# A two-layer hybrid decoder on one core: down tiles and input-projection parts laid out so that the last four activations come later, and ada loads issued ahead

## The chip, the cores and the metric

The kernel runs on one core of a Trainium2 chip. The time is device time in microseconds of one execution. Three runs of the kernel before took 996.03, 997.90 and 997.75 us, median 997.75. The engines named below are TensorE (PE, with its weight loads as PEld), VectorE (DVE), ScalarE (ACT), GpSimd (POOL) and SyncE (SP), which issues nearly all loads.

## What is computed

Two layers, 256 tokens of width 1024, all in float32. Each layer is a half-step SwiGLU, a mixer of latent attention and a gated short convolution, and another half-step SwiGLU. Each sublayer's norm is modulated by shift, scale and gate, which come from the conditioning vector c through a matrix w_ada of 9 x 1024 columns per layer:

```python
def swiglu(h, w_gu, w_down):
    g, u = jnp.split(h @ w_gu, 2, axis=-1)
    return (jax.nn.silu(g) * u) @ w_down

c_act = jax.nn.silu(c)
for l in range(DEPTH):
    mod = jnp.split(c_act @ w_ada[l] + b_ada[l], N_MOD, axis=-1)
    h = modulate(rms_norm(x, ffn1_norm[l]), mod[0], mod[1])
    x = x + FFN_RESIDUAL * (1 + mod[2])[:, None, :] * swiglu(h, ffn1_w_gu[l], ffn1_w_down[l])
    h = modulate(rms_norm(x, mix_norm[l]), mod[3], mod[4])
    y = hybrid_mixer(h, cos, sin, w_in[l], q_a_norm[l], w_uq[l], kv_a_norm[l], w_ukv[l],
                     conv_w[l], attn_out_norm[l], conv_out_norm[l], w_o[l])
    x = x + (1 + mod[5])[:, None, :] * y
    h = modulate(rms_norm(x, ffn2_norm[l]), mod[6], mod[7])
    x = x + FFN_RESIDUAL * (1 + mod[8])[:, None, :] * swiglu(h, ffn2_w_gu[l], ffn2_w_down[l])
return rms_norm(x, final_norm)
```

## The kernel before

**Weights.** All weights come in chunks of 128 x 2048 float32 (1 MB), 16 tiles of 128 x 128. A chunk is loaded by SP into `raw`, copied by ACT to `hi` in the matmul's reduced float format (L262), and VectorE forms `lo` = raw - hi (L265). TensorE then makes each product in three passes: hi by hi, hi by lo, lo by hi, all recorded at L287. The activations are split in the same way: `u` is the modulated norm's input of a sublayer (hi at L351 on ACT, lo at L357 on VectorE), `a` the SwiGLU product between gate/up and down (L351, L355). raw, hi and lo have three buffers each, PSUM has four.

**Sublayers.** An ffn takes 22 gate/up chunks, one per 128 columns of gate and of up, and then 11 down chunks: 8 output blocks (m0 to m7), each a sum over 22 activation blocks (k0 to k21), 22 tiles per block. When a block is summed, VectorE adds it to x with a gate (residual, L394), and ACT and VectorE form the next sublayer's u of that block at once, and its square for the norm's sum (acc, L322). The mixer follows a list, ORDER, of parts: K, Q, P, c and d are parts of the input projection of four tiles each (d the last columns of the convolution), q, s, t and a belong to attention, A and B to the output projection, N, Z, V, X, L, v to the latent's expansion, m and n are the sums of the two output norms, and w means that the next weight chunk is taken up here, ahead of its use.

**Modulation.** The product with w_ada is made on VectorE: 144 blocks of 128 rows, 512 KB each, are loaded by SP into `ada` (four buffers) and reduced by one instruction each (L189). A table, PACE, says how many must be done by which weight chunk.

**What sets the order.** SP's program order is written out: for each chunk its raw load and then the ada loads that PACE wants by then; inside the mixer TensorE's order is also written out. On VectorE and ACT a scheduler orders the work by due times (`due`), which run with TensorE's modelled clock, and by when it expects its inputs. Each engine executes in its own order, so whatever stands behind a waiting instruction waits too. The lines that the steps below touch are `load` (L235 to L276), `ffn` (the loop over `KD * NJ` tiles), `proj` (parts of four tiles), the output projection's residuals and the packing of dn and win.

Of the kernel before, what the change touches and what calls it, by code (L numbers as in the profile page):

```python
# [18 lines left out]
P = 128  # L19
L = 2  # L20
D = 1024
S = 256
KD = D // P
# [8 lines left out]
CH = 16 * P  # L32
WHOLE = 4
ADA_SLACK = 10000
ROPE_SLACK = 20000
LATE = 4
PACE = (0, 0), (8, 16), (21, 32), (33, 58), (49, 64), (84, 97), (117, 130), (133, 136), (146, 144)
LOAD_LEAD, SPLIT_LEAD, URGENT = 12000, 3000, 0
ENGS = {'p': mybir.EngineType.PE, 's': mybir.EngineType.SP, 'v': mybir.EngineType.DVE, 'a': mybir.EngineType.Activation}
MAN = 'sp'  # L40
SM_ACT = 2
ORDER = ("K K K X K Q Q P Q Q P P L c c c P c N Z V v q0 q1 s0 q2 c c c c t0 s1 a0 q3 c c c t1 c a1 s2 s3 c c c c t2 d d a2 t3 d d a3 "
         "d n w d w d d A A A w m A A w A A A B B B B B B B B").split()
WIN = dict(K=0, Q=1, P=2, c=3, d=7)
WO = dict(A=0, B=2)
SLACK = {'B': 6000, 'K': -2000, 'L': -4000, 'N': 0, 'P': 6000, 'Q': 0, 'V': 1000, 'X': 6000, 'Z': -4000, 'a': -4000, 'c': 6000, 'd': 0, 'm': 6000, 'n': 0, 'q': 2000, 's': -6000, 't': -4000}
# [1 line left out]
GUARD = ('m',)  # L48
MIX_SPLIT, MIX_ADA = 2000, 2000
GU_SLACK, DN_SLACK = 3000, 4000  # L50
NA = 72
SCALE = 96.0 ** -0.5
NEG = -1.0e30
# [66 lines left out]
def trunk(ctx: ExitStack, tc, x_d, c_d, pos_d, small_d, cst_d, ada_d, gu1_d, dn1_d, win_d, up_d, wo_d, gu2_d, dn2_d, out_d):  # L120
# [89 lines left out]
    stream = []  # L210
    for l in range(L):
        stream += [(gu1_d[l, j], CH, 2, WHOLE * P if l == 0 and j < 8 else 0) for j in range(NJ)]
        stream += [(dn1_d[l, j], CH, 2) for j in range(11)]
        up = {t: (up_d[l, :, a:a + n], n, 2) for t, a, n in (("N", 0, CH), ("q0", CH, 1536), ("q2", CH + 1536, 768),
                                                           ("q3", CH + 2304, 768))}
        n = {}
        for t in ORDER:
            n[t] = n.get(t, -1) + 1
            if t in up:
                stream.append(up[t])  # L220
            elif t in WIN and n[t] % 4 == 0:
                stream.append((win_d[l, WIN[t] + n[t] // 4], CH, CUTS))
            elif t in WO and n[t] % 4 == 0:
                stream.append((wo_d[l, WO[t] + n[t] // 4], CH, CUTS))
        stream += [(gu2_d[l, j], CH, 2) for j in range(NJ)]
        stream += [(dn2_d[l, j], CH, 2) for j in range(11)]
    taken = [0]

    ready = []
# [5 lines left out]
    def load(apart=False, head=False):  # L235


        i = taken[0]
        taken[0] += 1
        src, n, cuts = stream[i][:3]  # L240
        z0 = stream[i][3] if len(stream[i]) > 3 else 0
        raw = wp.tile([P, CH], F32, tag="raw", name=nm("raw"), bufs=3)
        hi = wp.tile([P, CH], F32R, tag="hi", name=nm("hi"), bufs=3)
        lo = wp.tile([P, CH], F32R, tag="lo", name=nm("lo"), bufs=3)
        if head:
            ada_load(1)
            nc.sync.dma_start(raw[:, :z0], src[:, :z0])
            ada_load(2)
            nc.sync.dma_start(raw[:, z0:n], src[:, z0:n])
        else:  # L250
            due(-LOAD_LEAD)
            nc.sync.dma_start(raw[:, :n], src)
            due(lead[1])
            with ExitStack() as es:
                for q in guard:
                    es.enter_context(tc.issue_after(q))
                ada(ada_target(i + 1))
        c = (n - z0) // cuts
        zs = [slice(z0 + q * c, z0 + (q + 1) * c) for q in range(cuts)]

        def top(q):
            nc.scalar.activation(hi[:, zs[q]], raw[:, zs[q]], AF.Copy)  # L262

        def rest(q):
            nc.vector.tensor_tensor(lo[:, zs[q]], raw[:, zs[q]], f32(hi[:, zs[q]]), ALU.subtract)  # L265

        if apart:
            return (raw, hi, lo), top, rest
        with ExitStack() as es:
            for q in guard:  # L270
                es.enter_context(tc.issue_after(q))
            for q in range(cuts):
                due(c / 128 * 322 * q - lead[0])
                top(q)
                rest(q)
        return raw, hi, lo  # L276
# [127 lines left out]
    def ffn(l, sub, pre, nxt, first=False):  # L404
# [132 lines left out]
                evac(j, pt[:, 0, :S], pt[:, 1, :S], None)  # L537
        if nxt is None:
            y = [wk.tile([P, 4, S], F32, tag="ada", name=nm("y"), bufs=4) for _ in range(2)]
        for t in range(KD * NJ):  # L540
            m, k = divmod(t, NJ)
            if t % 16 == 0:
                w = chunk()
            if k == 0:
                ps = ps_tile()[:, 0, :]
            if m < KD - 1:
                mm3w(ps, w, t % 16, aB[k], aH[k], k == 0, k == NJ - 1)
            else:
                mm3(ps, w, t % 16, aH[k], aL[k], k == 0, k == NJ - 1)
            if k == NJ - 1:  # L550
                due(DN_SLACK if m < KD - 1 else -URGENT)
                residual(ps, m, l, sub, 0.5, m < KD - 1)
                if nxt is None:
                    if m == KD - 1:
                        psf = ps_tile()[:, 0, :S]
                        fin.sums(psf, True, False)
                        due(-URGENT)
                        fin.acc = None
                    fin.add(x[:, m, :])
                    nc.scalar.activation(y[m // 4][:, m % 4, :], x[:, m, :], AF.Copy, scale=small[:, L * SM_L + m:L * SM_L + m + 1])  # L560
                    if m == KD - 1:
                        last_norm(psf, y)
                else:
                    nxt.put(m)
                    if m == 5:
                        nxt.shifts()

    def mixer(l, pre, nxt):
# [35 lines left out]
        def proj(t, evac):  # L604

            n = seen[t] = seen.get(t, -1) + 1
            if n % 4 == 0:
                open_[t] = chunk(), ps_tile()
            w, pt = open_[t]
            i = n % 4 // 2  # L610
            for k in range(n % 2 * 4, n % 2 * 4 + 4):
                mm3(pt[:, i, :], w, i * KD + k, uH[:, k, :], uL[:, k, :], k == 0, k == KD - 1, 2)
            if n % 4 == 3:
                due(SLACK[t])
                evac(scaled(pt))
# [163 lines left out]
        def out(t):  # L779
# [13 lines left out]
                dst = acc[m // 2 % 2][:, g, (m % 2) * S:(m % 2 + 1) * S]  # L793
                mm3(dst, w, m % 4 * 4 + k, zH[:, k, :], zL[:, k, :], half == 0 and k == 0 and m % 2 == 0, half == 1 and k == 3)
            if half == 1 and i % 2 == 1:
                due(SLACK["B"])
                for q in (i - 1, i):
                    m = 4 * g + q
                    residual(acc[m // 2 % 2][:, g, (m % 2) * S:(m % 2 + 1) * S], m, l, 1, 1.0)
                    nxt.put(m)  # L800
                    if m == 5:
                        nxt.shifts()
# [101 lines left out]
def _layout(a):  # L904
# [18 lines left out]
    for f in (1, 2):  # L923
# [3 lines left out]
            head = w[0, :8].reshape(8, P, 8, 2, P).transpose(2, 1, 0, 3, 4).reshape(1, 8, P, CH)  # L927
            w = np.concatenate([np.concatenate([head, w[:1, 8:]], axis=1), w[1:]], axis=0)
        g[f"gu{f}"] = np.ascontiguousarray(w)
        t = _tiles(a[f"ffn{f}_w_down"]).transpose(0, 2, 1, 3, 4).reshape(L, 11, 16, P, P)  # L930
        g[f"dn{f}"] = np.ascontiguousarray(t.transpose(0, 1, 3, 2, 4).reshape(L, 11, P, CH))
    w = a["w_in"]
    kv, kpe, q = w[:, :, QR:QR + KVR], w[:, :, QR + KVR:QR + KVR + 32], w[:, :, :QR]
# [3 lines left out]
    for i, s in [(i, s) for i in range(4) for s in (1, 2)] + [(i, 0) for i in range(4)]:  # L937
        parts.append(w[:, :, o + s * CW + i * P:o + s * CW + (i + 1) * P])
    t = _tiles(np.concatenate(parts, axis=2))
    t = t.transpose(0, 2, 1, 3, 4).reshape(L, 9, 16, P, P)  # L940
    g["win"] = np.ascontiguousarray(t.transpose(0, 1, 3, 2, 4).reshape(L, 9, P, CH))
    uk = a["w_ukv"].reshape(L, 2, P, H, 128)
    nope = uk[..., :64].reshape(L, 2, P, 4, P).transpose(0, 2, 3, 1, 4).reshape(L, P, 1024)
# [30 lines left out]
```

## Time and profile before

| what | value |
|---|---|
| median of three runs | 997.75 us |
| the profiled execution's own time | 1002.27 us |
| span of its profile | 1000.5 us |
| TensorE busy | 977.1 us, 98% |
| VectorE busy | 854.1 us, 85% |
| ACT busy | 581.3 us, 58% |
| granted TensorE clock, mean | 0.994 |
| loads | 248.59 MB, 250 GB/s over the span |

The profile is one execution, and its time lies 1.8 us over its span and 4.5 us over the median. Layer 0's first ffn takes the first 205 us, with its down from 144; the mixer is from 205 to 312; the second ffn to 501; layer 1 repeats this, with its mixer from 689 and its second ffn from 801. The release named behind an idle time is inferred from semaphores. In a row of a timeline the first number is the start in us, the second the duration; operations that follow each other without a gap are put together, with xN.

### The profile page before, as it was taken

Reading aid. Unit: us, or ns where it says so; the run is one execution under the profiler, and the core shown is the slowest. Engines: PE = TensorE matmul, PEld = TensorE weight load, DVE = VectorE, ACT = ScalarE, POOL = GpSimd, SP = SyncE. Lnnn points to the kernel's source line nnn. Section 1 sums busy time; section 2 is a strip of 40 time slices with the busy share of each in tenths; the row PEclk is TensorE's granted clock in tenths of the full one; section 3 lists DMA queues with packets and bytes.
Section 4 is the critical chain, followed back from the end, with each engine's and each line's share of the span. In section 5 each row is a group of like instructions: output and inputs, shape, how many; then the busy total and the mean of one; then the engine's idle time right before and its main releaser. Section 6 shows DMA issues by size and latency. Waiting matters only on the chain.

```text
span 1000.5 us, 16812 instructions
## 1 busy us (share of the span) xinstructions
PE 977.1 (98%) x6560; PEld 898.1 (90%) x6560; DVE 854.1 (85%) x1598; ACT 581.3 (58%) x1010; POOL 8.0 (1%) x27
## 2 busy tenths in 40 slices
PE   9999999999999999999999999998999999999996
PEld 7999998899989988888998888888998998888885
DVE  5899999999999998988899878877799999766653
ACT  4465544467856755654486555543687676656541
POOL 0000110000000000000000000000000000000000
PEclk9999999999999999999999999998999999999998
DMA  9999998874746687877768777776355547655531
GB/s 348 376 361 340 336 320 324 311 282 154 275 178 253 234 318 253 301 267 291 270 219 324 279 258 283 277 255 214 124 217 193 200 171 290 215 178 201 173 122 43
DMA packets 47007, 250.78 MB, mean 251 GB/s; under 512 B 5504, under 2 KB 5824, under 8 KB 26576
## 3 DMA queue, kind: packets, MB, share of 16 engines
q1 hardware_dynamic: 46224, 248.81, 68.3%
q8 instruction: 51, 0.84, 0.3%
q10 hardware_dynamic: 288, 0.65, 0.2%
q0 software_dynamic: 416, 0.25, 0.1%
q14 instruction: 28, 0.23, 0.1%
HBM read 248.59 MB, written 1.10 MB: 250 GB/s over the span
## 4 chain that ended last, share of the span: by engine, by line
PE 78%; DVE 11%; DMA 7%; issue 1%; ACT 1%; SPq 0%; DVEq 0%; ACTq 0%
PE ps L287 78%; DMA ada<-in_ada 6%; DVE lo L265 5%; DVE ada L189 1%; DVE x L394 1%; DMA raw<-in_gu 1%; DVE acc L322 1%; DVE u L357 1%; PE ps L731 1%; DVE mr L355 1%; ACT hi L262 0%; DMA cb<-in_c 0%; DVE nt L594 0%; ACT mr L351 0%; DVE mf L767 0%
## 5 line engine op out<-in xcount | busy, mean ns | idle before, releaser
L287 PE MATMUL ps<-u,hi 128*128 128x256 f32 (+2 forms) x2464 | 599.8, 324 | 6.5 <-ACT u L351 3.7
L287 PE MATMUL ps<-u,lo 128*128 128x256 f32 (+1 forms) x1664 | 470.1, 283 | 1.1 <-DVE lo L265 1.1
L287 PEld LDWEIGHTS ps<-u,hi 128*128 128x128 f32 x2464 | 413.5, 190 | 46.4 <-ACT u L351 4.3
L265 DVE TENSOR_TENSOR lo<-raw,hi 128x1024 fp32r<-128x1024 f32 (+2 forms) x384 | 394.8, 1046 | 41.4 <-ACT hi L262 40.9
L262 ACT ACTIVATE hi<-raw 128x1024 fp32r<-128x1024 f32 (+2 forms) x384 | 338.3, 912 | 113.4 <-PE ps L287 48.9
L287 PEld LDWEIGHTS ps<-u,lo 128*128 128x128 f32 x1664 | 315.9, 190 | 1.4 <-DVE lo L265 1.4
L287 PE MATMUL ps<-a,hi 128*128 128x512 f32 (+1 forms) x792 | 248.6, 372 | 1.4 <-DVE a L355 1.4
L189 DVE CUSTOM_DVE_ANT_0 ada<-ada,cb,small 128x1024 f32<-128x1024 f32 x144 | 183.1, 1280 | 33.4 <-DMA ada<-in_ada 32.8
L287 PE MATMUL ps<-a,lo 128*128 128x256 f32 x704 | 197.9, 281 | 0.0
L287 PEld LDWEIGHTS ps<-a,hi 128*128 128x128 f32 x792 | 143.0, 189 | 29.8 <-DVE a L355 1.7
L287 PEld LDWEIGHTS ps<-a,lo 128*128 128x128 f32 x704 | 133.2, 189 | 0.0
L351 ACT ACTIVATE a<-cc 128x256 fp32r<-128x256 f32 x88 | 36.3, 415 | 68.0 <-DVE cc L413 56.3
L287 PE MATMUL ps<-mr,hi 128*128 128x256 f32 x384 | 70.6, 285 | 0.0
L351 ACT ACTIVATE u<-x,gs 128x256 fp32r<-128x256 f32 x40 | 20.3, 507 | 84.6 <-DVE x L394 84.6
L287 PEld LDWEIGHTS ps<-mr,hi 128*128 128x128 f32 x384 | 60.2, 192 | 0.8 <-issue 0.3
L287 PE MATMUL ps<-mr,lo 128*128 128x256 f32 x192 | 54.3, 283 | 0.0
L394 DVE SCALAR_TENSOR_TENSOR x<-ps,gate,x 128x256 f32<-128x256 f32 x76 | 35.9, 480 | 19.2 <-PE ps L287 18.5
L355 DVE TENSOR_TENSOR a<-cc,a 128x256 fp32r<-128x256 f32 x88 | 37.0, 422 | 16.0 <-ACT a L351 15.8
L412 ACT ACTIVATE cc<-g 128x256 f32<-128x256 f32 x54 | 22.5, 418 | 41.5 <-DVE g L411 41.5
L411 DVE TENSOR_TENSOR g<-ps,g 128x512 f32<-128x512 f32 x54 | 37.0, 685 | 0.7 <-ACT g L410 0.6
L287 PEld LDWEIGHTS ps<-mr,lo 128*128 128x128 f32 x192 | 36.8, 191 | 0.0
L410 ACT ACTIVATE g<-ps 128x512 f32<-128x512 f32 x54 | 31.2, 578 | 0.0
(121 smaller groups left out, 568.4 us busy)
## 6 DMA issues: line engine op xcount, KB each, us to landing
raw<-in_gu SPq DMA_DIRECT2D x87, 1024.0 KB, 5.8
ada<-in_ada SPq DMA_DIRECT2D x144, 512.0 KB, 6.2
raw<-in_dn SPq DMA_DIRECT2D x44, 1024.0 KB, 5.2
raw<-in_win SPq DMA_DIRECT2D x18, 1024.0 KB, 5.7
raw<-in_wo SPq DMA_DIRECT2D x8, 1024.0 KB, 4.8
raw<-in_up SPq DMA_DIRECT2D x2, 1024.0 KB, 5.9
raw<-in_up SPq DMA_DIRECT2D x2, 768.0 KB, 4.4
raw<-in_up SPq DMA_DIRECT2D x4, 384.0 KB, 3.1
```

Source lines behind the costliest of these rows:

```text
L189: nc.vector.tensor_tensor_reduce(out=a, in0=a, in1=cb, scale=1.0, scalar=sm(l, t), op0=ALU.mult, op1=ALU.add, accum_out=mods[l][:, t:t + 1])
L262: nc.scalar.activation(hi[:, zs[q]], raw[:, zs[q]], AF.Copy)
L265: nc.vector.tensor_tensor(lo[:, zs[q]], raw[:, zs[q]], f32(hi[:, zs[q]]), ALU.subtract)
L287: nc.tensor.matmul(dst, a, b, **kw)
L322: nc.vector.tensor_tensor(self.acc, self.acc, t, ALU.add)
L351: nc.scalar.activation(dH, src, AF.Copy, scale=scale)
L355: nc.vector.tensor_tensor(dL, src, f32(dH), ALU.subtract)
L357: nc.vector.scalar_tensor_tensor(dL, src, scale, f32(dH), ALU.mult, ALU.subtract)
L394: nc.vector.scalar_tensor_tensor(x[:, m, :], s, g, x[:, m, :], ALU.mult, ALU.add)
L410: nc.scalar.activation(t2, pg[:, :, :S], AF.Copy)
L411: nc.vector.tensor_tensor(t2, pg[:, :, S:], t2, ALU.add)
L412: nc.scalar.activation(sg, t2[:, 0, :], AF.Silu)
```

## The change

Five edits. A chunk's ada loads stand ahead of its raw load on SP, and reach two blocks further than PACE asks (ADA_AHEAD). Down's tiles are in a new order: m0 and m1 first sum k0 to k17, then both k18 to k21; the other blocks as before. The weights are packed to suit. A down chunk is split by one operation of 2048 columns on ACT and on VectorE, no longer two of 1024. In the input projection, the first two parts of a chunk now take k0 to k3 of both its column blocks and the last two k4 to k7, also packed to suit; in ORDER, two Q parts stand between the second and the third K, and further on one w is dropped and the d parts move behind a3. Last, the residuals that are wanted at once get a due time 1500 earlier (URGENT), the output projection's last pair among them.

```diff
+ADA_AHEAD = 2
-LOAD_LEAD, SPLIT_LEAD, URGENT = 12000, 3000, 0
+LOAD_LEAD, SPLIT_LEAD, URGENT = 12000, 3000, 1500
-ORDER = ("K K K X K Q Q P Q Q P P L c c c P c N Z V v q0 q1 s0 q2 c c c c t0 s1 a0 q3 c c c t1 c a1 s2 s3 c c c c t2 d d a2 t3 d d a3 "
-         "d n w d w d d A A A w m A A w A A A B B B B B B B B").split()
+ORDER = ("K K Q Q K X K Q Q P P P L c c c P c N Z V v q0 q1 s0 q2 c c c c t0 s1 a0 q3 c c c t1 c a1 s2 s3 c c c c t2 d d a2 t3 d a3 "
+         "d d n d w d d A A A w m A A w A A A B B B B B B B B").split()
+DOWN = [(m, k) for k0, k1 in ((0, 18), (18, NJ)) for m in (0, 1) for k in range(k0, k1)] + [
+    (m, k) for m in range(2, KD) for k in range(NJ)]
...
-        stream += [(dn1_d[l, j], CH, 2) for j in range(11)]
+        stream += [(dn1_d[l, j], CH, 1) for j in range(11)]
...
             due(-LOAD_LEAD)
+            if not apart:
+                ada_load(min(ada_target(i + 1) + ADA_AHEAD, len(ADA_ORDER)))
             nc.sync.dma_start(raw[:, :n], src)
...
-        for t in range(KD * NJ):
-            m, k = divmod(t, NJ)
+        pd = {}
+        for t, (m, k) in enumerate(DOWN):
             if t % 16 == 0:
                 w = chunk()
             if k == 0:
-                ps = ps_tile()[:, 0, :]
+                pd[m] = ps_tile()[:, 0, :]
+            ps = pd[m]
...
-            i = n % 4 // 2
-            for k in range(n % 2 * 4, n % 2 * 4 + 4):
-                mm3(pt[:, i, :], w, i * KD + k, uH[:, k, :], uL[:, k, :], k == 0, k == KD - 1, 2)
+            i, h = n % 2, n % 4 // 2
+            for k in range(4 * h, 4 * h + 4):
+                mm3(pt[:, i, :], w, 4 * (n % 4) + k % 4, uH[:, k, :], uL[:, k, :], k == 0, k == KD - 1, 2)
...
-                due(SLACK["B"])
+                due(SLACK["B"] if n < 7 else -URGENT)
```

Three places show how the instructions move. The first is SP's queue at gate/up chunk 8 of layer 0 (`raw_84`), the first chunk to which the new order of loads applies. Before:

```order
26 L252 DMA raw_70_592<-in_gu1 128x2048
27 L252 DMA raw_84_687<-in_gu1 128x2048
28 L180 DMA ada_87_691<-in_ada 128x1024
29 L252 DMA raw_90_752<-in_gu1 128x2048
30 L180 DMA ada_93_756<-in_ada 128x1024
```

Now three ada loads stand ahead of it. The third needs a buffer that VectorE's reduction of ada_68 frees:

```order
26 L257 DMA raw_70_592<-in_gu1 128x2048
27 L183 DMA ada_87_690<-in_ada 128x1024
28 L183 DMA ada_88_692<-in_ada 128x1024
29 L183 DMA ada_89_694<-in_ada 128x1024
30 L257 DMA raw_84_687<-in_gu1 128x2048
31 L183 DMA ada_95_759<-in_ada 128x1024
```

VectorE at the same place, where lo_86 is the lo of that chunk, cc and `a` are the evacuations of the chunk before it, and L192 are reductions. Before, lo_86 stood right behind lo_72 and ahead of the first cc. Now:

```order
79 L270 TENSOR_TENSOR lo_72_594<-raw_70_592,hi_71_593 128x768
80 L421 TENSOR_TENSOR cc_76_647<-ps_18_157,cc_76_647 128x256
81 L192 ISA ada_88_692,mod0_88<-ada_88_692,cb_72,small_73 128x1024
82 L192 ISA mod0_88 128x1
83 L360 TENSOR_TENSOR a_74_645<-cc_76_647,a_74_645 128x256
84 L421 TENSOR_TENSOR cc_77_652<-ps_18_157,cc_77_652 128x256
85 L421 TENSOR_TENSOR cc_78_657<-ps_19_158,cc_78_657 128x256
86 L192 ISA ada_89_694,mod0_88<-ada_89_694,cb_72,small_73 128x1024
88 L360 TENSOR_TENSOR a_74_645<-cc_77_652,a_74_645 128x256
89 L360 TENSOR_TENSOR a_74_645<-cc_78_657,a_74_645 128x256
90 L421 TENSOR_TENSOR cc_79_662<-ps_19_158,cc_79_662 128x256
91 L270 TENSOR_TENSOR lo_86_689<-raw_84_687,hi_85_688 128x1024 x2
```

The chunk's split has moved behind two reductions and the evacuations of four columns.

The second is VectorE in layer 0's first down, at the first residual (m0: it adds ps_183 before, ps_185 now; each residual is two instructions, one to x and one more with the same gate for the other half of the products). lo_194 is down chunk 2 in both, lo_202 before and lo_204 now chunk 3. Before:

```order
249 L265 TENSOR_TENSOR lo_194_1779<-raw_192_1777,hi_193_1778 128x1024
250 L381 TENSOR_TENSOR u_75<-mod0_88,u_75 128x8
251 L394 SCALAR_TENSOR_TENSOR x_71<-ps_183_1688,gate_189_1747,x_71 128x256 x2
252 L265 TENSOR_TENSOR lo_202_1836<-raw_200_1834,hi_201_1835 128x1024
253 L357 SCALAR_TENSOR_TENSOR u_75<-x_71,gs_2_91,u_75 128x256
254 L265 TENSOR_TENSOR lo_202_1836<-raw_200_1834,hi_201_1835 128x1024
255 L189 ISA ada_203_1838,mod0_88<-ada_203_1838,cb_72,small_73 128x1024
```

Now:

```order
249 L270 TENSOR_TENSOR lo_194_1770<-raw_192_1768,hi_193_1769 128x2048
250 L192 ISA ada_206_1837,mod0_88<-ada_206_1837,cb_72,small_73 128x1024
251 L192 ISA mod0_88 128x1
252 L377 SCALAR_TENSOR_TENSOR gs_3_92<-mod0_88,small_73 128x1
253 L399 SCALAR_TENSOR_TENSOR x_71<-ps_185_1690,gate_197_1796,x_71 128x256
254 L270 TENSOR_TENSOR lo_204_1834<-raw_202_1832,hi_203_1833 128x2048
255 L399 SCALAR_TENSOR_TENSOR x_71<-ps_185_1690,gate_197_1796,x_71 128x256
256 L399 SCALAR_TENSOR_TENSOR x_71<-ps_191_1739,gate_199_1813,x_71 128x256
257 L192 ISA ada_210_1879,mod0_88<-ada_210_1879,cb_72,small_73 128x1024
```

The chunk's lo still follows the residual of m0, but that residual now needs down's tile 40, where it needed tile 22.

The third is VectorE where layer 1 goes from down to the mixer. lo_969 before and lo_963 now is the second chunk of the mixer, and the residual of ps_943 or ps_945 is down's last, m7. Before:

```order
1077 L265 TENSOR_TENSOR lo_969_7511<-raw_967_7509,hi_968_7510 128x512 x4
1078 L189 ISA ada_989_7657,mod1_89<-ada_989_7657,cb_72,small_73 128x1024
1079 L189 ISA mod1_89 128x1
1080 L394 SCALAR_TENSOR_TENSOR x_71<-ps_943_7331,gate_948_7409,x_71 128x256
1081 L265 TENSOR_TENSOR lo_973_7548<-raw_971_7546,hi_972_7547 128x512 x2
1082 L357 SCALAR_TENSOR_TENSOR u_75<-x_71,gs_701_5560,u_75 128x256
```

Now:

```order
1055 L192 ISA ada_991_7594,mod1_89<-ada_991_7594,cb_72,small_73 128x1024
1056 L192 ISA mod1_89 128x1
1057 L270 TENSOR_TENSOR lo_963_7404<-raw_961_7402,hi_962_7403 128x512 x4
1058 L399 SCALAR_TENSOR_TENSOR x_71<-ps_945_7271,gate_950_7347,x_71 128x256
1059 L270 TENSOR_TENSOR lo_979_7525<-raw_977_7523,hi_978_7524 128x512 x2
1060 L362 SCALAR_TENSOR_TENSOR u_75<-x_71,gs_703_5520,u_75 128x256
```

The reduction stands ahead of the second chunk's lo, no longer between it and the last residual.

More of the change, by code (lines that the diff above doesn't have):

```diff
@@ L225, in trunk @@
         stream += [(gu2_d[l, j], CH, 2) for j in range(NJ)]
-        stream += [(dn2_d[l, j], CH, 2) for j in range(11)]
+        stream += [(dn2_d[l, j], CH, 1) for j in range(11)]
     taken = [0]
@@ L929, in _layout @@
         g[f"gu{f}"] = np.ascontiguousarray(w)
-        t = _tiles(a[f"ffn{f}_w_down"]).transpose(0, 2, 1, 3, 4).reshape(L, 11, 16, P, P)
+        t = _tiles(a[f"ffn{f}_w_down"])
+        t = np.stack([t[:, k, m] for m, k in DOWN], axis=1).reshape(L, 11, 16, P, P)
         g[f"dn{f}"] = np.ascontiguousarray(t.transpose(0, 1, 3, 2, 4).reshape(L, 11, P, CH))
@@ L939, in _layout @@
     t = _tiles(np.concatenate(parts, axis=2))
-    t = t.transpose(0, 2, 1, 3, 4).reshape(L, 9, 16, P, P)
+    t = t.transpose(0, 2, 1, 3, 4).reshape(L, 9, 2, 2, 4, P, P).swapaxes(2, 3).reshape(L, 9, 16, P, P)
     g["win"] = np.ascontiguousarray(t.transpose(0, 1, 3, 2, 4).reshape(L, 9, P, CH))
```

## The prediction

> **What bounds the kernel now.** I read the page's busy time first, then the waits of TensorE, then windows by stage. The page's busy rows (engine, busy us, share of the span):
>
> ```profile
> PE 977.1 (98%) x6560; PEld 898.1 (90%) x6560; DVE 854.1 (85%) x1598; ACT 581.3 (58%) x1010; POOL 8.0 (1%) x27
> ```
>
> TensorE is idle for 1000.5 - 977.1 = 23.4 us, and the arithmetic does not change. So the change can only move these 23.4 us, the time lost to a lower clock, and new waits. VectorE's 85% is the second number to hold on to. What TensorE waits for (us in total, times, the longest):
>
> ```profile
> PE ps L287 <- ACT u L351: 3.7, 3, 2.6
> PE ps L287 <- DVE acc L322: 3.3, 4, 1.5
> PE ps L287 <- DVE u L357: 2.7, 3, 1.0
> PE ps L287 <- DVE a L355: 1.4, 1, 1.4
> PE ps L287 <- DVE lo L265: 1.1, 1, 1.1
> ```
>
> They are activations that come late: u where a sublayer starts, `a` between gate/up and down, norm sums (acc), one weight's lo. Windows (length, then the busy time of PE, PEld, DVE, ACT, POOL, the granted clock, DMA share, GB/s) put them in their places:
>
> ```profile
> 60.00:144.00 84.00, 84.00 (x708) 84.00 (x707) 79.69 (x166) 44.12 (x75) 6.72 (x13) 1.00 0.92 337
> 144.00:200.00 56.00, 56.00 (x331) 49.64 (x330) 53.22 (x95) 25.66 (x37) 0.00 (x0) 1.00 0.85 322
> ...
> 690.00:702.00 12.00, 8.74 (x46) 8.16 (x46) 6.17 (x13) 3.44 (x8) 0.00 (x0) 0.72 0.52 168
> 695.06:701.89 6.83, 6.16 (x27) 5.93 (x27) 3.47 (x9) 1.80 (x4) 0.00 (x0) 0.50 0.38 115
> ```
>
> Two stages matter. From 690 to 702, where layer 1 goes from down to the mixer, TensorE idles 3.26 us and then runs at half clock for 6.83 us. From 144 to 200, layer 0's first down, TensorE never waits, but VectorE is busy 53.22 of 56 us: it has 2.8 us in hand.
>
> **The gains, part by part.** Layer 1, down to mixer. VectorE's timeline there:
>
> ```profile
> 692.44 1.28 DVE L189 CUSTOM_DVE_ANT_0 ada<-ada,cb,small 128x1024 f32<-128x1024 f32 x1 [2.74 <-DMA ada<-in_ada]
> ...
> 693.65 0.48 DVE L394 SCALAR_TENSOR_TENSOR x<-ps,gate,x 128x256 f32<-128x256 f32 x1
> ...
> 695.25 0.48 DVE L357 SCALAR_TENSOR_TENSOR u<-x,gs,u 128x256 fp32r<-128x256 f32 x1
> 695.64 0.42 DVE L322 TENSOR_TENSOR acc<-acc,sq 128x256 f32<-128x256 f32 x1
> 695.98 0.68 DVE L265 TENSOR_TENSOR lo<-raw,hi 128x512 fp32r<-128x512 f32 x1
> ```
>
> The last residual (693.65) stands behind an ada reduction that waits 2.74 us for its load. Two edits hit this. The load goes ahead of a raw chunk, so it no longer queues behind that chunk's wait on SP. And the last four activations are wanted four parts after the mixer's start (5.8 us, four parts of four tiles at 0.36 us each) instead of one part after it. Last u ready at 695.25 + 0.48 = 695.7 now; without the 2.74 it is 693.0, and TensorE, which started the mixer at 689.5, would ask for it after 695. The whole loss goes: 3.26 us idle, and 12 x (1 - 0.72) = 3.4 us of clock. Gain 6.6 us. If the reduction still waited its 2.74 us, last u at 695.7 would meet a demand at 695.3 to 696.4, so some 0.4 us would stay; I take 6.6.
>
> [...]
>
> Layer 0, down to mixer, on TensorE:
>
> ```profile
> 205.44 0.40 PE L287 MATMUL ps<-u,hi 128*128 128x258 f32 x2
> 206.99 0.39 PE L287 MATMUL ps<-u,lo 128*128 128x258 f32 x1 [1.14 <-DVE lo L265]
> ```
>
> A tile's lo pass starts 0.24 us after its hi passes, so 206.99 is 1.31 us late. The mixer's first lo waits behind three ada reductions and the last residual; in the new order it stands ahead of that residual. Gain 1.3 us, in exchange for the loss below. The norm sums before the last two conv columns: of the 3.3 us in four waits the longest is 1.5, and I give two long ones 1.45 each, one per layer; the two d parts now put between a3 and n cover them (a part is 1.44 us): 2.9 us. Gate/up to down in layer 1: the last four activations are wanted 36 tiles of 0.35 us = 12.5 us after down's start, not 6.2 us: 1.4 us. Start of ffn2: of the u waits, 3.7 + 2.7 - 3.26 = 3.1 us lie at its two starts; the last residual now has a due time 1500 earlier, but still follows TensorE's last part, and I take 0.9 us of the 3.1 (0 to 3.1). Sum of gains: 6.6 + 1.3 + 2.9 + 1.4 + 0.9 = 13.1 us. They are not sure to be independent; with all but the first at half they are 9.9.
>
> **The losses: layer 0's down.** In the new order the reductions ahead of the lo of a given down chunk there are five more than before, and the first residual waits for tile 40 of down, not tile 22, with the next chunk's lo queued right behind it. VectorE cannot use its free time before tile 40, so what counts is what it has to do from there. TensorE's side:
>
> ```profile
> 144.05 0.39 PE L287 MATMUL ps<-a,hi 128*128 128x512 f32 x1
> ...
> 199.58 0.40 PE L287 MATMUL ps<-a,hi 128*128 128x256 f32 x2
> ```
>
> 144.05 is down's first tile and 199.58 its tile 160, where the last chunk begins: 0.347 us a tile. Tile 40 ends at 157.9, so TensorE has 41.65 us of work until it needs the last chunk's lo. VectorE's rows in that stretch, start to start:
>
> ```profile
> 63.27 1.22 DVE L265 TENSOR_TENSOR lo<-raw,hi 128x1024 fp32r<-128x1024 f32 x1
> 64.41 0.42 DVE L355 TENSOR_TENSOR a<-cc,a 128x256 fp32r<-128x256 f32 x1
> ...
> 202.76 1.28 DVE L189 CUSTOM_DVE_ANT_0 ada<-ada,cb,small 128x1024 f32<-128x1024 f32 x1
> 203.97 0.08 DVE L189 DVE_READ_ACCUMULATOR2_ANT mod<- 128x1 f32 x1
> ...
> 205.17 0.15 DVE L392 TENSOR_SCALAR gate<-mod 128x1 f32<-128x1 f32 x1
> 205.24 0.15 DVE L372 SCALAR_TENSOR_TENSOR gs<-mod,small 128x1 f32<-128x1 f32 x1
> ```
>
> A 1024 split takes 1.14 us (63.27 to 64.41), a reduction 1.21, a one-column operation 0.07 to 0.08; from the rows at 693.65 to 695.98 a residual takes 0.40, u 0.39, acc 0.34. The groups by shape give the size of a split without its wait:
>
> ```profile
> L265 DVE TENSOR_TENSOR lo<-raw,hi 128x1024 fp32r<-128x1024 f32 x252 | 304.9, 1219 | 37.3 <-ACT hi L262 37.2
> L265 DVE TENSOR_TENSOR lo<-raw,hi 128x512 fp32r<-128x512 f32 x104 | 67.1, 684 | 0.3
> ```
>
> 512 more columns cost 1219 - 684 = 535 ns, so the one split of 2048 takes 1.14 + 2 x 0.535 = 2.21 us (2.28 as two; no trace of before has one, and 2.0 to 2.4 moves the sum by 1.6 either way). The new order has, from the first residual to the last chunk's lo: 8 splits x 2.21 = 17.7, 16 reductions x 1.21 = 19.4, 14 residuals x 0.40 = 5.6, 6 u x 0.39 = 2.3, 5 acc x 0.34 = 1.7, 13 small ones x 0.08 = 1.0: 47.7 us. TensorE falls behind by 47.7 - 41.65 = 6.1 us, in waits for lo of 2 to 3 us at chunk five of down and less at each after it. Ends: 0 if five of the reductions slip to where VectorE waits anyhow, and 9 if VectorE also waits 1.1, 1.1 and 0.6 us for the third to sixth accumulations.
>
> [...] Two splits here would have the half that TensorE needs first ready 1.1 us earlier, a loss of 5.0, and the time 992; no run here shows it yet.
>
> **The loss at chunk 8.** This is the first chunk with its ada loads ahead of it. Three go ahead on SP, the third needs a buffer that a reduction frees at 54 us, and the raw chunk, issued at 48 before, stands behind it. The schedule answers by putting its split behind four evacuations and two more reductions. From ACT's and VectorE's rows there, and TensorE's first use:
>
> ```profile
> 59.94 0.39 ACT L415 ACTIVATE cc<-ps 128x256 f32<-128x256 f32 x1 [0.57 <-PE ps L287]
> ...
> 60.73 0.42 DVE L416 TENSOR_TENSOR cc<-ps,cc 128x256 f32<-128x256 f32 x1
> 61.07 1.27 DVE L189 CUSTOM_DVE_ANT_0 ada<-ada,cb,small 128x1024 f32<-128x1024 f32 x1
> ...
> 64.05 0.41 PE L287 MATMUL ps<-u,hi 128*128 128x256 f32 x2
> 64.30 0.28 PE L287 MATMUL ps<-u,lo 128*128 128x256 f32 x1
> ```
>
> The first evacuation's Silu ends at 60.33. Behind it VectorE does four cc and three `a` at 0.34, from 60.73 to 61.07 (2.4), and two reductions at 1.21 (2.4): 65.1, plus 1.2 for the first half: lo at 66.3 against a use at 64.30. Loss 2.0 us; 0 if the scheduler's evacuations come sooner, 3.5 if the raw chunk lands after 64.
>
> **Sum.** -13.1 + 6.1 + 2.0 = -5.0 us. The profiled execution's own time is 1002.27 us (span 1000.5), so 997.3 by its rows; it lies 4.5 us over the median of the runs, 997.75, and I take the difference over: 992.75, said as 993. Everything else is hidden: the permuted layouts move the same bytes, the longer ACT copies of down chunks lie in an engine that is 46% busy from 144 to 200 (25.66 of 56.00), and K's and Q's lo, now both wanted in the first 5.8 us, take 8 x 0.6 = 4.8 us ahead of the last residual, whose u TensorE asks for 5.8 us after the mixer's start (if they are late the 1.3 us comes back). One early take-up (w) of an output weight less costs a 0.6 us split at most; I take 0.
>
> **Rivals.** First, VectorE keeps up in layer 0 because its reductions run in gaps that I counted as lost. For it: 2.8 free us from 144 to 200 and 4.3 in the 84 us before. Against it: the residual's place ahead of a lo. Then only about 1 us is lost: 997.75 - 13.1 + 1 = 985.7 us.
>
> Second, slower: SP's queue chains the raw chunks to VectorE. Each ada load ahead needs a buffer freed by a reduction, VectorE is late from chunk 8 on, so each raw chunk is issued later, its split comes later, and VectorE, which has idle time only while it waits for a split, loses that too. It decides once the lead of lo over use is gone; price: 2.0 + 9 + the 7.1 us of idle VectorE time between 60 and 200 that is no longer recovered = 18.1, less 13.1: +5, hence 1002 to 1003. Against it: the loads fill 0.85 of the DMA engines' time from 144 to 200, less than the 0.92 before, so a late one can catch up.
>
> Third, no change: the wait for an ada load and the half clock at 690 to 702 are of the profiled execution, which is 4.5 us over the median, and ordinary runs have little of it. Then 4.5 of the 6.6 is no gain: 997.3.
>
> **How the numbers follow.** Forecast 0.50, VectorE keeps up 0.20, SP's chain 0.17, gain only in the profile 0.13. A measurement of this kernel can tell about 0.2%, 2 us. The forecast's own spread, 988 to 998, is 0.85 faster, 0.12 same, 0.03 slower; the second is all faster; SP's chain is slower for 0.85 of it; the last is half same, the rest split. Faster 0.65, same 0.15, slower 0.20. The range 984 to 1002 takes in the second case and most of the third.
>
> **What would show it.** Right: a wait for lo of about 2 us near 64 and some 6 us of waits for lo between 160 and 205; none for acc over 0.5; no clock under 0.9 near 690. Wrong: no lo waits in layer 0 (first rival); raw loads in layer 0 issued only when a reduction ends, with the split waiting on ACT's hi and that on the DMA (second). The forecast falls if layer 1's start of the mixer still waits over 2 us, or down loses over 9 us.

## The result and the profile after

The change made the kernel slower: 1009.24 us median of four runs (1007.84 to 1010.73), against 997.52 in the runs beside them; ratio 1.0119, 95% interval 1.0099 to 1.0139. The forecast was 993.

| | before | after |
|---|---|---|
| median of the runs | 997.52 us | 1009.24 us |
| the profiled execution's own time | 1002.27 us | 1010.73 us |
| span of its profile | 1000.5 us | 1008.9 us |
| TensorE busy | 977.1 us | 983.0 us |
| VectorE busy | 854.1 us | 847.8 us |
| mean granted clock | 0.994 | 0.988 |

What TensorE waits for in the changed kernel (us in total, times, the longest):

```profile
PE ps L292 <- DVE u L386: 7.1, 2, 4.0
PE ps L292 <- DVE lo L270: 3.0, 5, 1.2
PE ps L292 <- DVE gate L397: 2.0, 1, 2.0
...
PE ps L292 <- ACT hi L267: 0.9, 2, 0.6
```

The waits of before for u, acc and `a` are nearly gone. At the head stands a name that was in no list of before: L386, an operation on 8 columns that writes the shifts, the last column of u. The windows of the changed kernel (length, then busy PE, PEld, DVE, ACT, POOL, clock, DMA share, GB/s) say where:

```profile
60.00:70.00 10.00, 8.28 (x56) 7.86 (x56) 9.63 (x20) 6.62 (x15) 0.00 (x0) 0.85 1.01 404
...
160.00:213.00 53.00, 48.86 (x274) 41.71 (x273) 49.60 (x82) 22.11 (x28) 0.00 (x0) 0.97 0.81 307
...
320.00:336.00 16.00, 12.94 (x94) 12.72 (x93) 14.44 (x38) 6.18 (x14) 0.00 (x0) 0.89 0.44 168
...
640.00:705.00 65.00, 64.97 (x407) 58.38 (x407) 54.08 (x86) 33.07 (x44) 0.00 (x0) 1.00 0.74 261
...
800.00:820.00 20.00, 15.96 (x111) 15.61 (x110) 18.98 (x41) 10.69 (x20) 0.00 (x0) 0.83 0.48 187
```

Layer 1's way into the mixer, which begins at 699.90 here, has lost its idle time, to 705 as the row shows and on to 715. Four places are new or worse. Each has idle time and a clock under 1.00: 1.7 us idle and 10 x 0.15 = 1.5 us of clock near chunk 8; 4.1 and 1.6 in layer 0's down; 3.1 and 1.8 where layer 0's second ffn starts; 4.0 and 3.4 where layer 1's does. That is 21 us, of which before had 3 in the last two places. It is what one execution shows: of the four runs the profiled one has the lowest mean clock, 0.988 against 0.991 to 0.994. A mean of 0.994 over 1008.2 us leaves room for 12.1 us at half clock, less than the 17.1 us of the four stretches shown at the end of this document, so not every stretch of low clock comes in every run.

The start of layer 0's second ffn on VectorE:

```profile
308.88 6.03 DVE L270 TENSOR_TENSOR lo<-raw,hi 128x512 fp32r<-128x512 f32 x9
314.83 0.87 DVE L399 SCALAR_TENSOR_TENSOR x<-ps,gate,x 128x256 f32<-128x256 f32 x2
...
321.51 1.40 DVE L399 SCALAR_TENSOR_TENSOR x<-ps,gate,x 128x256 f32<-128x256 f32 x3
...
324.35 0.47 DVE L399 SCALAR_TENSOR_TENSOR x<-ps,gate,x 128x256 f32<-128x256 f32 x1
324.75 0.16 DVE L386 TENSOR_TENSOR u<-mod,u 128x8 fp32r<-128x8 f32 x1
```

And TensorE's first row of that ffn:

```profile
325.06 0.47 PE L292 MATMUL ps<-u,hi 128*128 128x258 f32 x2 [3.06 <-DVE u L386]
```

The 258 columns of the first pass hold the shifts, so even the first of 22 chunks cannot begin without them. Their operation needs no recent input. It stands behind eight residuals because VectorE, from 308.88 on, has a train of nine splits to do and is behind with everything.

In layer 0's down VectorE now waits once for 4.2 us, with the lo of down's fourth chunk behind it; afterwards TensorE waits:

```profile
161.84 0.48 DVE L399 SCALAR_TENSOR_TENSOR x<-ps,gate,x 128x256 f32<-128x256 f32 x1 [4.23 <-PE ps L292]
162.24 2.28 DVE L270 TENSOR_TENSOR lo<-raw,hi 128x2048 fp32r<-128x2048 f32 x1
164.44 0.87 DVE L399 SCALAR_TENSOR_TENSOR x<-ps,gate,x 128x256 f32<-128x256 f32 x2
```

```profile
170.36 2.28 DVE L270 TENSOR_TENSOR lo<-raw,hi 128x2048 fp32r<-128x2048 f32 x1
172.57 0.14 DVE L397 TENSOR_SCALAR gate<-mod 128x1 f32<-128x1 f32 x1
...
172.70 0.58 PE L292 MATMUL ps<-a,lo 128*128 128x256 f32 x1 [1.95 <-DVE gate L397]
```

The releaser named there is a gate, the operation just behind the split in VectorE's queue; the tile it waits for is lo, of down's fifth chunk, whose split ends at 172.64.

### The profile page after: what moved, and what is told of

Same layout as the page of the kernel before. It is cut to its first block, busy times and chain, and to the rows that moved or that the text cites. A ratio compares the mean times of both kernels' runs of the same rounds, so it can differ in the third digit from the quotient of the medians.

```text
span 1008.9 us, 16751 instructions
## 1 busy us (share of the span) xinstructions
PE 983.0 (97%) x6560; PEld 902.3 (89%) x6560; DVE 847.8 (84%) x1554; ACT 577.7 (57%) x966; POOL 8.0 (1%) x27
## 4 chain that ended last, share of the span: by engine, by line
PE 88%; DVE 8%; DMA 1%; issue 1%; ACT 1%; DVEq 0%; SPq 0%; ACTq 0%
PE ps L292 87%; DVE lo L270 3%; DVE ada L192 2%; DMA raw<-in_gu 1%; DVE x L399 1%; PE ps L737 1%; DMA cb<-in_c 0%; DVE u L362 0%; DVE nt L600 0%; DVE mr L360 0%; DVE acc L327 0%; DVE rs_a L348 0%; DVE rs_a L347 0%; ACT hi L267 0%; DVE y L406 0%
## 5 line engine op out<-in xcount | busy, mean ns | idle before, releaser
L270 DVE TENSOR_TENSOR lo<-raw,hi 128x1024 fp32r<-128x1024 f32 (+4 forms) x340 | 388.8, 1162 | 43.6 <-ACT hi L267 43.2
L267 ACT ACTIVATE hi<-raw 128x1024 fp32r<-128x1024 f32 (+4 forms) x340 | 331.5, 1005 | 116.9 <-PE ps L292 50.2
L192 DVE CUSTOM_DVE_ANT_0 ada<-ada,cb,small 128x1024 f32<-128x1024 f32 x144 | 183.2, 1280 | 29.5 <-DMA ada<-in_ada 29.4
```

The lines of the kernel that those rows point to most:

```text
L192: nc.vector.tensor_tensor_reduce(out=a, in0=a, in1=cb, scale=1.0, scalar=sm(l, t), op0=ALU.mult, op1=ALU.add, accum_out=mods[l][:, t:t + 1])
```

## The experiments

Times are medians; ratios are to the kernel before in the same batch, whose medians were 996.75 to 998.45. The changed kernel was not run again, so a difference to it, and most differences between two versions, are between batches, and are good to some 2 us.

**The w put back.** The edit, in ORDER:

```diff
-"d d n d w d d A A A w m A A w A A A B B B B B B B B"
+"d d n d w d w d d A A A w m A A w A A A B B B B B B B B"
```

(The row of before is `d n w d w d d`; the changed one has a single w between n and A, and here there are two again.)

> The changed kernel with one entry of ORDER put back: a w between the fourth d and the last three, so that the third output-projection chunk is taken up ahead of its use again. Nothing else differs. Theory: the two new waits at the starts of the second ffn (TensorE waits 3.1 us and 4.0 us there for the column of shifts, L386) come from that missing w: the chunk's split falls behind the norm of the convolution, VectorE has a backlog into the output projection, and the shift, which needs nothing recent, is ordered behind it. Then both waits go, with the half clock behind them (3.4 and 6.8 us long): 8 to 10 us less than the changed kernel's 1009.2, so 999 to 1001. Rival: the shift is late because the last pair of residuals is due 1500 early and passes the fifth; then w changes under 2 us, 1007 to 1009.

1001.3 us, ratio 1.0044 (1.0027 to 1.0061): 8 us less than the changed kernel, and just over the expected 999 to 1001. Its TensorE waits from 300 to 830:

```profile
PE ps L292 <- DVE acc L327: 1.8, 2, 1.0
PE ps L292 <- DVE lo L270: 1.5, 2, 0.8
PE ps L292 <- ACT mr L356: 0.3, 1, 0.3
```

No wait for L386 is left. In the order of this kernel the shift stands some 40 rows earlier, among the norm sums, and the train of splits ahead of the residuals has five in place of nine:

```profile
310.20 3.63 DVE L270 TENSOR_TENSOR lo<-raw,hi 128x512 fp32r<-128x512 f32 x5
```

The missing w makes the loss at the second ffns; the first theory held.

**The loads as before.** The three lines that load ada ahead of raw are taken out:

```diff
-            if not apart:
-                ada_load(min(ada_target(i + 1) + ADA_AHEAD, len(ADA_ORDER)))
```

> The changed kernel with the ada loads behind the raw load and only as far as PACE asks, as before. Theory of the prediction: the reductions that stand ahead of the splits in layer 0 cost 2.0 us at chunk 8 and some 5 of the 7 us lost from 160 to 213; without them both go, and the reduction's wait for its load at layer 1's mixer returns but is hidden by the later demand: 1009.2 - 3.7 - 5 = 1000 to 1002. Rival: the residual that waits for tile 40 is what stops VectorE in layer 0's down; then only chunk 8's 2 to 4 us go: 1005 to 1007.

1000.94 us, ratio 1.0027 (1.0008 to 1.0046): 8.3 us less. TensorE's waits from 60 to 215, all of them, and VectorE's from 140 to 215:

```profile
PE ps L290 <- DVE lo L268: 0.2, 1, 0.2
```

```profile
DVE x L397 <- PE ps L290: 2.6, 1, 2.6
```

VectorE still waits for tile 40, now 2.6 us, and TensorE loses nothing by it. So the residual's wait alone costs nothing; it needs the extra reductions to turn it into a loss. Layer 1's mixer starts without a wait here too (60.00 of 60.00 us busy from 640 to 700): the early loads were not needed for that.

**Down as before.** Tiles in plain order, two splits per chunk:

```diff
-DOWN = [(m, k) for k0, k1 in ((0, 18), (18, NJ)) for m in (0, 1) for k in range(k0, k1)] + [
-    (m, k) for m in range(2, KD) for k in range(NJ)]
+DOWN = [(m, k) for m in range(KD) for k in range(NJ)]
...
-        stream += [(dn1_d[l, j], CH, 1) for j in range(11)]
+        stream += [(dn1_d[l, j], CH, 2) for j in range(11)]
...
```

> The changed kernel with down's tiles in plain order (m0 complete after 22 tiles) and down's chunks split in two operations, as before. Rival of the run without the ahead loads: if the wait of the first residual for tile 40 makes the loss of layer 0's down, 5 to 7 us go there and the 1.4 us wait between gate/up and down in layer 1 returns: 1003 to 1006. If it is the reductions ahead, the loss in layer 0's down stays at 5 or more and the time is 1008 to 1011.

1006.02 us, ratio 1.0077 (1.0050 to 1.0105): 3.2 us less. From 60 to 215 TensorE waits 3.1 us for lo and 1.4 for hi, and the wait between gate/up and down in layer 1 is back with 2.5 us. The time is at the edge of the first expectation (1003 to 1006), but its mechanism is only half there: from 160 to 213 TensorE still idles 2.8 us, where the changed kernel has 4.1 us and a clock of 0.97 (over the whole execution the mean clock is 0.990 here and 0.988 there). So the reductions alone keep part of the loss, and the late residual adds to it.

**The order of the parts as before.** ORDER, `proj` and the packing of win are those of the kernel before, the rest stays changed:

```diff
-            i, h = n % 2, n % 4 // 2
-            for k in range(4 * h, 4 * h + 4):
+            i = n % 4 // 2
+            for k in range(n % 2 * 4, n % 2 * 4 + 4):
```

> The changed kernel with ORDER and the parts of the input projection as before (k0 to k7 of one column block in two parts); down, loads, split and due times stay changed. Theory: the w comes back with it, so the waits for shifts at both second ffns go (8 to 10 us); the last activations at the mixer's start are wanted early again: 1 to 3 us in each layer come back, and 1.5 us per layer for the norm sums: 1002 to 1006. Rival (due times): the waits for shifts stay, 1010 to 1014.

1006.67 us, ratio 1.0087 (1.0057 to 1.0116). The waits for the shift are gone with the w, as in the first run. The norm sums wait again, six times, 4.7 us together, and `a` waits 2.0 us from 640 to 720. The time is 0.7 us over the first expectation (1002 to 1006), and one part of that did not come: no u is waited for from 640 to 720, although it is wanted early again.

**Both undone.** The w is back and the loads are as before; down's order, its single split, the parts of the input projection and the due times stay.

> The changed kernel with both suspects undone: the w put back in ORDER and the ada loads behind the raw loads as before. Down's tile order, one split per down chunk, the parts of the input projection and the due times stay changed. If the two losses are separate and all of the loss, this keeps every gain: from the changed kernel 8 us for the ada loads (as measured with them alone undone) and 8 us for the w (as measured): 1009.2 - 8.3 - 7.9 = 993, and by the stages of the traces (start to start times over the usual ones: 26 us against 36.5 before) 988 to 990. Rival: the gains seen in single stages of profiled executions are of the profile, and the kernel is at 996 to 999, the same as before.

989.37 us, ratio 0.9919 (0.9888 to 0.9950): 8 us faster than before and 20 faster than the change as it came. It is called the fastest version below. The mean clock of its profiled execution is 0.998, and it is 1.00 from 60 to 72, 140 to 200, 300 to 326, 640 to 700 and 785 to 812. TensorE's waits from 60 to 980:

```profile
PE ps L290 <- DVE acc L325: 1.8, 2, 1.0
PE ps L290 <- DVE a L358: 1.5, 1, 1.5
PE ps L290 <- DVE u L360: 0.8, 1, 0.8
PE ps L290 <- ACT mr L354: 0.5, 2, 0.3
PE ps L290 <- DVE lo L268: 0.2, 1, 0.2
```

Without the dropped w and the early loads, what is left of the change is a gain.

Four of these kernels have TensorE's work in the same order but for a few matmuls, so the first tile of each down dates their stages. The table gives its start in the fastest version, and how many us later it starts in the others, in the profiled executions:

| | layer 0, first down | layer 0, second down | layer 1, first down | layer 1, second down |
|---|---|---|---|---|
| fastest version, start | 143.64 | 435.60 | 623.67 | 916.75 |
| loads ahead, w back | 4.9 | 13.8 | 12.5 | 11.5 |
| loads as before, w dropped | -0.1 | 6.6 | 5.3 | 10.5 |
| changed kernel | 4.1 | 15.7 | 14.4 | 19.3 |

The early loads lose all that they lose in layer 0; with the w back they win 2.3 us of it back later. The dropped w loses once in each layer, between the first down and the second.

**The w dropped from the kernel before.**

```diff
-"d n w d w d d A A A w m A A w A A A B B B B B B B B"
+"d n w d d d A A A w m A A w A A A B B B B B B B B"
```

> The kernel before with the same w taken out of ORDER and nothing else. Its shift is ordered ahead of the fifth and sixth residuals, not behind all. If the missing w alone makes the loss at the second ffn, it costs 3 to 4 us per layer here too: 1004 to 1007. If it takes the early due time of the last pair as well to push the shift to the end, the cost here is the wait for the split and a shorter wait for the shift, 0.5 to 2 us per layer: 999 to 1002.

1002.15 us, ratio 1.0036 (1.0012 to 1.0060). TensorE waits from 300 to 375 for u, not for the shift:

```profile
PE ps L287 <- ACT u L351: 1.2, 2, 1.0
PE ps L287 <- DVE u L357: 1.1, 1, 1.1
```

The backlog is there, and it costs 5.1 us by the medians (1 to 6 by the interval). The time is at the upper edge of the second expectation (999 to 1002). Of its mechanism one half holds: without the early due time the shift is not last. The shorter wait for it did not come; the wait is for u.

**The ahead loads in the kernel before.** The two lines of the second experiment are added to it.

> The kernel before with the ada loads ahead of the raw load and two blocks further, and nothing else: m0 of down is still complete after 22 tiles and is split in two operations. By the run without the ahead loads they cost 4 us near chunk 8 and 6 us in layer 0's down. If that needs no other part of the change, the same is lost here, less up to 4 us that the earlier load saves at layer 1's mixer: 1002 to 1008. If it takes the residual behind tile 40 to turn the extra reductions into waits, only the 4 us near chunk 8 are lost: 996 to 1002.

1001.97 us, ratio 1.0055 (1.0027 to 1.0083). Its windows:

```profile
60.00:72.00 12.00, 10.28 (x84) 9.86 (x83) 11.46 (x21) 8.01 (x17) 0.00 (x0) 1.00 1.02 411
160.00:212.00 52.00, 49.10 (x293) 42.40 (x292) 49.37 (x89) 22.81 (x34) 0.00 (x0) 1.00 0.87 333
640.00:700.00 60.00, 60.00 (x384) 54.57 (x383) 49.57 (x87) 29.60 (x49) 0.00 (x0) 1.00 0.74 258
```

1.7 us idle near chunk 8 and 2.9 in down, with down's plain order and two splits. The time lies where the two expectations meet, so the windows decide: with m0 complete after 22 tiles, TensorE waits for lo in down all the same. The loads need no other part of the change to do harm. They also clear layer 1's start of the mixer, and still lose.

**The last pair due as before**, with the w still missing:

```diff
-                due(SLACK["B"] if n < 7 else -URGENT)
+                due(SLACK["B"])
```

> The changed kernel with the last pair of the output projection's residuals due as before, so that they no longer pass the fourth and fifth; the w stays dropped. If the early due time is what sends the shift behind all residuals, the waits of 3.1 and 4.0 us for it go down to under 1.5 each and their half clock goes: 1002 to 1005. If the backlog from the missing w is enough, over 2.5 us of wait stay at each start: 1007 to 1010.

1008.03 us, ratio 1.0100 (1.0067 to 1.0134), 1.2 us less than the change, with overlapping ranges. The shift is now ordered ahead of the last residuals and nobody waits for it, but TensorE waits for u at the same place, 1.2 + 1.1 us, with the half clock behind it (0.89 from 320 to 336, as in the changed kernel). The second expectation was right in its time (1007 to 1010) and nearly in its waits, 2.3 us at this start and 2.2 at layer 1's, just under its 2.5. The due time decides which operation comes last and adds 0.8 and 1.8 us of wait; the rest of the wait belongs to the backlog.

**The kernel before once more.**

> The kernel before once more, unchanged, for a second profiled execution. The one shown took 1002.27 us, 4.5 over the median, with 3.3 us of waits and 6.8 us of half clock at layer 1's mixer (690 to 702). If that stage is the same in every execution, it is here again: 6 to 7 us lost from 640 to 720. If it hangs on when one ada load lands, it is smaller here by 2 us or more, and that part of the forecast's gain was of the profile.

999.3 us. The window that the prediction showed of its first profile:

```profile
690.00:702.00 12.00, 10.22 (x81) 9.76 (x81) 9.76 (x20) 6.71 (x15) 0.00 (x0) 1.00 0.42 145
```

1.8 us idle from 690 to 702 and full clock, where the first profile had 3.3 us idle and a clock of 0.72. The reduction ahead of the last residual waits 1.86 us for its load here, 2.74 there. So of the 6.6 us that I counted as a gain, 4.8 are not in this second execution.

**Two splits, from the fastest version.** Only the count of splits in down chunks goes back to 2.

> The fastest version so far (w back, ada loads as before: 989.4) with down chunks split in two operations again, as before the change. VectorE's extra cost is 0.07 us for each of 44 chunks on an engine that is 85% busy; TensorE never waited for a lo in down there. Theory: no difference, 988 to 991. Rival: one split frees VectorE enough where it is full, and two cost 1 to 3 us: 990.5 to 992.5.

990.19 us, ratio 0.9913 (0.9880 to 0.9946): no difference that these runs can tell, in a version in which VectorE is not behind in down.

**Only the order of the parts and the due times, from the fastest version.** Down's order and splits are as before too.

> The fastest version so far (w back, ada loads as before: 989.4) with down's tiles in plain order and two splits: what is left of the change is the order of the parts of the input projection and the due times. Down's order can only save the waits between gate/up and down and in VectorE's queue behind the residual: 1 to 3 us, so 990.5 to 992.5. Rival: the reduction's late load makes the wait between gate/up and down in layer 1 (1.5 us) with either order, and the order of down is worth nothing: 988.5 to 990.5.

993.19 us, ratio 0.9941 (0.9913 to 0.9970), over both expectations. The wait between gate/up and down in layer 1 is 3.7 us in its profiled execution, whose mean clock is 0.995, against 0.998 in the fastest version's. Down's order is worth 3 to 4 us by the medians; the intervals of the two ratios overlap.

**The ahead loads from layer 0's mixer on**, with the w back. Chunk 33 is the mixer's first.

```diff
-            if not apart:
+            if i >= 33:
                 ada_load(min(ada_target(i + 1) + ADA_AHEAD, len(ADA_ORDER)))
```

> The fastest version so far with the ada loads ahead of the raw loads from the first chunk of layer 0's mixer on, and as before in layer 0's first ffn, where VectorE has no time to spare. Theory: the ahead loads hurt only where VectorE is the bound; later they take away VectorE's waits for loads, 1.65 us between gate/up and down and 1.1 us at layer 1's start: 986 to 989. Rival: they fill VectorE's queue ahead of the splits at layer 0's second ffn too, as waits for lo near 340 and 370 in the changed kernel with the w back show: 990 to 993.

994.67 us, ratio 0.9960 (0.9938 to 0.9981): 5 us slower than without them, where I expected a gain. TensorE's waits from 60 to 980:

```profile
PE ps L292 <- DVE lo L270: 2.9, 4, 1.2
PE ps L292 <- DVE acc L327: 1.8, 2, 0.9
PE ps L292 <- DVE mr L360: 0.6, 1, 0.6
```

The waits for `a` and u of the fastest version are gone, as expected. Four waits for lo have come in their place; 1.5 us of them lie in layer 0's second ffn (300 to 375). That is the rival's mechanism, at a time over its 990 to 993.

**The place of the loads alone** (ADA_AHEAD 0, the w back), and **their reach alone** (two blocks further, but behind their raw load, the w back). The edit of the second:

```diff
+            nc.sync.dma_start(raw[:, :n], src)
             if not apart:
                 ada_load(min(ada_target(i + 1) + ADA_AHEAD, len(ADA_ORDER)))
-            nc.sync.dma_start(raw[:, :n], src)
```

> The changed kernel with the w back, and the ada loads ahead of the raw load but only as far as PACE asks (ADA_AHEAD 0, not 2). With the w back it takes 1001.3, and 989.4 with the loads as they were before. If the 12 us are the price of the reach (two more blocks loaded, so two to five more reductions ahead of each split), most of it goes: 990 to 993. If they are the price of the place (the raw chunk queued on SP behind a load that needs a buffer from a reduction), most of it stays: 998 to 1002.

> The changed kernel with the w back, and the ada loads two blocks further than PACE asks, but behind their raw load as before the change. Price of the reach: most of the 12 us stays, 998 to 1002, since VectorE still meets the reductions ahead of the splits and the next raw chunk still queues behind the third load. Price of the place: 990 to 993.

994.38 us (ratio 0.9971, 0.9956 to 0.9986) and 992.29 (0.9939, 0.9914 to 0.9964), against 989.4 with neither and 1001.3 with both. Place costs 5.0 us, reach 2.9, together 11.9, more than their sum. The profiled executions show where the rest can lie: with both, layer 0's first ffn loses 3.3 us to a lower clock (0.86 from 60 to 72, 0.97 from 160 to 214), and the mean clock of the whole execution is 0.994; with the place alone it is 0.996, with the reach alone 0.998, as with neither. In the orders of the four kernels, 56 reductions stand ahead of the lo of down's last chunk with neither, 58 with the place or the reach alone, and 60 with both. TensorE's waits for lo from 60 to 215 are 0.2 us with neither, 2.8 with the place alone, 2.3 with the reach alone. The reach alone lies in the range for the price of the place (990 to 993), the place alone in neither. Both halves put reductions ahead of splits; that it is these reductions alone that cost, and nothing else that the loads move, is not shown.

## Why the prediction was wrong

It forecast -5 us, and the change was +11.7. By its own steps:

**"One early take-up (w) of an output weight less costs a 0.6 us split at most; I take 0."** This step failed, and it is the largest. I priced the dropped w as one split. What it moves is a whole chunk's split, four operations on ACT and four on VectorE, from beside the last projection parts to behind the convolution's norm, where the next chunks' splits follow. VectorE then starts the output projection with a train of splits (the 6.03 us row at 308.88), the residuals come late, and the start of the second ffn waits. The undone w is worth 7.9 us with the loads ahead and 1000.94 - 989.37 = 11.6 without them. The forecast is 16.7 us off, so this step is about half of it or more. I had even taken a gain of 0.9 us at this place, from a due time.

**The losses in layer 0.** The sum had 6.1 us for down and 2.0 for chunk 8, 8.1 together; taking the loads out of the changed kernel gives 8.3, but 11.9 once the w is back, so that the totals agree is in part luck. At each place the terms hold roughly: near chunk 8 TensorE's first lo of that chunk starts late by waits of 0.6 (hi) and 1.2 us (lo), 1.7 us idle in all for the 2.0; in down VectorE waits 4.2 us at the residual, and TensorE then idles 4.1 us from 160 to 213, for the 6.1. VectorE takes 49.5 us from the first residual to the end of the last chunk's lo (161.84 to 211.37), where the sum had 47.7. The half clock (1.5 and 1.6 us) was in no term; with it the places cost 3.2 and 5.7 us. The cause was named rightly in part: the extra reductions are needed, but the residual behind tile 40 is not needed for a loss, as the loads in the kernel before showed.

**The gain at layer 1's mixer, 6.6 us**, was there in full in the profiled execution (25.00 of 25.00 us busy from 690 to 715 after, clock 1.00), but 4.8 of it was of that execution of before, by the second one. This is the third rival, to which I gave 0.13; it came true together with the losses. Whichever edit is left alone, the order of the parts or the loads, the place is clear, so the term was also bought twice.

**The norm sums, 2.9 us**: the two waits of 1.5 us are gone; in their place stand two shorter ones for mr, on ACT, 0.5 us together. The term held within half a us. **Gate/up to down in layer 1, 1.4 us**: gone in the changed kernel, but 1.5 us in the fastest version and 3.7 with down's plain order. By four executions it hangs on when a load lands: a reduction waits 2.0 us for its load ahead of the 3.7 and 1.65 us ahead of the 1.5, 1.02 us (at 628.98) in the first profile of before, where `a` is waited for 1.4, and 0.4 us in the second, where `a` is waited for 0.9. That the term's size came out is luck.

**The single split** cost and gave nothing that the runs can tell, where VectorE is not behind. It takes 2.20 us start to start (162.24 to 164.44 above) for the 2.21 of the sum.

**Of the rivals**, the first, that VectorE keeps up, did not come: TensorE waits for lo in layer 0. The slower one had a chance of 0.17 and the mechanism of SP's queue, with 1002 to 1003. The sign was right. Part of its mechanism is there (the raw load of chunk 8 issued at 54.5 us, not 47.9; the place of the loads alone is worth 5.0 us), but it hardly reaches past layer 0's first ffn, and the time came out at 1009 because of the w.

**The range**, 984 to 1002, had no term for the half clock after a new wait, and no bound for the w. Neither of the two things by which the forecast was to fall came about (layer 1's start of the mixer is clear, and down lost less than 9 us): the step that failed had no sign of its own.

## What to carry to other kernels

An entry that takes a weight chunk up early is not worth its own operations but the place of the whole train behind it (7.9 and 11.6 us here, where one split was priced at 0.6): where an engine is nearly full, as VectorE with 24.44 of 26.00 us busy from 309 to 335 in the changed kernel, ask what stands last in its queue once the train is late, down to the 8-column operation that the next stage needs first. Loads issued earlier are not free either where the consumer is the busy engine (they cost 8.3 us here, and 11.9 with the w back): its queue can then hold the consumers ahead of the work that TensorE waits for, as with 60 reductions in place of 56 ahead of the lo of down's last chunk. And a gain read from one profiled execution wants a second one, where it rests on when a load lands: 4.8 of 6.6 us were not in the second here.

## What the runs showed of the hardware

In the profiled execution of the changed kernel, TensorE's clock stands at 0.50 in four stretches ahead of its last matmul:

```profile
66.91:70.33 3.42, 3.42 (x18) 3.42 (x18) 3.42 (x8) 2.15 (x4) 0.00 (x0) 0.50 1.01 367
172.73:176.14 3.41, 3.41 (x11) 3.02 (x12) 3.36 (x9) 1.91 (x2) 0.00 (x0) 0.50 0.94 372
326.32:329.74 3.42, 3.42 (x19) 3.42 (x17) 3.42 (x8) 0.00 (x0) 0.00 (x0) 0.50 0.20 23
807.60:814.43 6.83, 5.30 (x25) 5.33 (x26) 6.83 (x13) 2.28 (x6) 0.00 (x0) 0.50 0.01 2
```

Three last 3.41 to 3.42 us and one twice that, 6.83. Each goes with a wait of TensorE. The first has two ahead of it, of 0.6 and 1.2 us, which end at 64.72 and 66.39; it begins at 66.91, with 1.7 us of idle from 60 on. The second and the third begin at 172.73 and 326.32, behind a wait of 1.95 us that ends at 172.70 and one of 3.06 us that ends at 325.06. The long one begins inside a wait of 4.0 us, which ends at 809.13. A stretch of 3.4 us at a clock of 0.50 costs 1.7 us, as much as the shorter waits themselves. The four starts are 105.82, 153.59 and 481.28 us apart, which is 31, 45 and 141 times the length of one short stretch (105.82 / 31, 153.59 / 45 and 481.28 / 141 all give 3.41 us): in this execution the starts lie on one grid.

A stretch does not always come: with the same 1.7 us of idle near chunk 8, the kernel before with the loads ahead kept a clock of 1.00 from 60 to 72. What decides it, no run here shows.
